# A sixth tile for split weights, operands kept split in DRAM, and PSUM reads put first in the seven products

## The chip, the cores and the metric

The kernel runs on one core of a Trainium2 chip. The metric is the time of one execution on the device in microseconds (us), the median of three runs. The five engines of the core have queues of their own and meet at semaphores: TensorE (PE; its weight loads are PEld), VectorE (DVE), ScalarE (ACT), GpSimd (POOL) and SyncE (SP, which here only issues transfers). Matmuls accumulate in eight PSUM banks.

## What is computed

A decoder layer over 2048 tokens of width 1024, in float32. Two branches (a gated DeltaNet with four heads, a sliding-window attention with eight query heads) read one normalized projection; their outputs are merged by gates, and a SwiGLU feed-forward of inner width 2816 follows:

```python
merged = gates[:, :, 0] * (y_dn @ w_branch_dn[l]) + gates[:, :, 1] * (y_swa @ w_branch_swa[l])
x = x + merged @ w_out[l]
h2 = rms_norm(x, ffn_norm[l])
x = x + (jax.nn.silu(h2 @ w_gate[l]) * (h2 @ w_up[l])) @ w_down[l]
```

The change lies in the feed-forward: `h2 @ w_gate` and `h2 @ w_up`, and the tiles through which all weights come.

## The kernel before

**Blocks.** The 2048 tokens are worked off in four blocks of 512. Each block goes through projections with the DeltaNet cores beside them (`mixer`), the output projection (`wo`), and the feed-forward. The next block's attention projections and its attention (`window_start`, `swa`) run inside the feed-forward of the block before, so that VectorE and ACT have their work there too.

**Split operands.** A product of float32 is made of three matmuls of a narrower type: hi times hi, hi times lo, lo times hi. A raw weight half of 128 x 512 is loaded into a `wraw` tile (256 KB, `load_raw`, L159), ACT makes its `hi` (L169), and VectorE or POOL, in turn, its `lo` by a subtraction (L170); the two stand in one `whl` tile. In block 0 the split weights of most products are also stored to DRAM (`wk<-whl`, 512 KB, L182), and blocks 1 to 3 load them back ready (`load_kept`, `whl<-wk`, L187), without `wraw` and without a split. There are eight `wraw` and five `whl` tiles; a tile is filled when the one that used its buffer before has been read.

**Feed-forward units.** The 22 units of 128 inner columns are grouped in five parts (4, 4, 4, 4, 6 units); after each part the down product adds its share. Block 0 uses plain products (`ffn_eight`): gate with A11 and A12, up with A21 and A22 (quarters of the two weight units), and in `four` it also makes the sums S1 to S4 of these quarters (VectorE and POOL, L229, tile `ws`), which are stored raw. Blocks 1 to 3 use Strassen's scheme with seven products of half size (`ffn_seven`), in the order S2, A11, S1, S3, A12, A22, S4; block 3 does its first two units plainly (`PLAIN`). Each of the seven operands is loaded raw and split each time it is used (`seven`).

**Chained banks.** The seven products share three PSUM banks, Y, G and Z. Y gets S2*T2, is copied to `c[:, 1]` by ACT (`pc<-acc`), gets S3*T3 on top, is read by VectorE into `U[:, 1]` (`pu<-pc,acc`), and then A22*T4 is added. So PE may not start A22 before `pu` is read. In the same way the second use of G waits for a `pc` copy, and that of Z for `up<-pu,acc`.

**What sets the order.** PE's order is written out at build time by a driver with a rough estimate of times: the dense products in program order, with steps of the side chains (attention, DeltaNet, norms) put in when they should be ready. The other engines' lists are ordered by a scheduler by priority, program order and readiness; side steps are emitted with a priority of 300. `refill` loads the next block's normalized activations `h` back at the beginning of the last part's down product (`h<-hk`, sixteen transfers on ACT's queue); they had been parked in DRAM by `window_start`.

Line numbers are those of the profile. Most operations are recorded through one helper and have its line, L110; they are told apart by their tiles.

Of the kernel before, what the change touches and what calls it, by code (L numbers as in the profile page):

```python
# [8 lines left out]
F32 = mybir.dt.float32  # L9
F32R = mybir.dt.float32r  # L10
I32 = mybir.dt.int32
AF = mybir.ActivationFunctionType
ALU = mybir.AluOpType
# [6 lines left out]
TB = 512  # L20
# [7 lines left out]
FSPLIT = (4, 4, 4, 4, 6)  # L28
NU = 60
ND = 6  # L30
WR = 8
WB = 5
PLAIN = 2
PSUB = 2
LANES = 2
GATES_AT = 2
# [79 lines left out]
class Emitter:  # L116
# [40 lines left out]
    def load_raw(self, src, n=TB):  # L157
        raw = self.wp.tile([P, 528], F32, name="wraw", tag="wraw", bufs=WR)
        self.raw.sync.dma_start(out=raw[:, :n], in_=src)  # L159
        return raw[:, :n]  # L160

    def either(self):
        self.nsub += 1
        return self.raw.vector if self.nsub > 6 and self.nsub % PSUB else self.raw.gpsimd

    def split_raw(self, r, n=TB):
        t = self.wp.tile([P, 2, 528], F32R, name="whl", tag="whl", bufs=WB)
        hi, lo = t[:, 0, :n], t[:, 1, :n]
        self.raw.scalar.activation(hi, r, AF.Copy)  # L169
        self.either().tensor_tensor(out=lo, in0=r, in1=hi, op=ALU.subtract)  # L170
        return t
# [13 lines left out]
    def load_kept(self, d, n=TB):  # L185
        t = self.wp.tile([P, 2, 528], F32R, name="whl", tag="whl", bufs=WB)
        self.raw.sync.dma_start(out=t[:, :, :n].bitcast(F32), in_=d)  # L187
        return t
# [20 lines left out]
    def quad(self, keys, m, h):  # L209
        return self.w_all[UNITS[keys[m]]][:, h * TB:(h + 1) * TB]  # L210

    def four(self, keys):

        v, gp = self.raw.vector, self.raw.gpsimd
        got = {n: self.load_raw(self.quad(keys, m, h))
               for n, m, h in (("A11", 0, 0), ("A12", 0, 1), ("A21", 1, 0), ("A22", 1, 1))}
        self.store_kept()

        def group(m):
            hl = [[t[:, e, :TB].rearrange("p (a m) -> p a m", a=4) for e in range(2)]  # L220
                  for t in [self.split_raw(got["A%d%d" % (m + 1, h + 1)]) for h in range(2)]]
            return lambda k: (hl[k // 4][0][:, k % 4], hl[k // 4][1][:, k % 4])

        def sums():
            kept = self.kept[keys] = {}
            for n, x, y, op, eng in (("S1", "A21", "A22", ALU.add, v), ("S2", "S1", "A11", ALU.subtract, v),
                                     ("S3", "A11", "A21", ALU.subtract, gp), ("S4", "A12", "S2", ALU.subtract, gp)):
                got[n] = self.u([TB], name="ws")
                eng.tensor_tensor(out=got[n], in0=got[x], in1=got[y], op=op)  # L229
                kept[n] = self.keep(got[n], [TB])  # L230
        return group, sums

    def seven(self, keys):

        own = {"A11": (0, 0), "A12": (0, 1), "A22": (1, 1)}
        self.store_kept()

        def of(name):
            t = self.split_raw(self.load_raw(self.quad(keys, *own[name]) if name in own else self.kept[keys][name]))
            return [t[:, e, :TB].rearrange("p (a m) -> p a m", a=4) for e in range(2)]  # L240
        return of

# [777 lines left out]
    def ffn_up(self, b, H, hs, f):  # L1020

        keys = (("up", f, 0), ("up", f, 1))
        if b == 0:
            group, sums = self.four(keys)
        elif b + 1 == self.nblocks and f < PLAIN:
            group, sums = lambda m: self.raw_weights(keys[m]), lambda: None
        else:
            return self.ffn_seven(H, keys)
        return self.ffn_eight(hs, group, sums)
# [28 lines left out]
    def ffn_seven(self, H, keys):  # L1058


        nc, v, gp = self.nc, self.nc.vector, self.nc.gpsimd
        yield lambda: len(H) == 4
        w = self.seven(keys)
        half = (slice(0, 256), slice(256, 512))
        bank = lambda: self.acc()[:, 0:256]
        Y = bank()
        yield from self.product(Y, w("S2"), H, "T2")
        c = self.u([2, 256], name="pc")
        nc.scalar.activation(c[:, 1], Y, AF.Copy)
        G = bank()  # L1070
        yield from self.product(G, w("A11"), H, "B11")
        nc.scalar.activation(c[:, 0], G, AF.Copy)
        U = self.u([2, 256], name="pu")
        gp.tensor_tensor(out=U[:, 0], in0=c[:, 0], in1=c[:, 1], op=ALU.add)
        Z = bank()
        yield from self.product(Z, w("S1"), H, "T1")
        yield from self.product(Y, w("S3"), H, "T3", start=False)
        v.tensor_tensor(out=U[:, 1], in0=c[:, 0], in1=Y, op=ALU.add)
        th = self.u([TB], name="th")
        up = self.u([TB], name="up")  # L1080
        v.tensor_tensor(out=up[:, half[1]], in0=U[:, 1], in1=Z, op=ALU.add)
        yield from self.product(G, w("A12"), H, "B21", start=False)
        nc.scalar.activation(th[:, half[0]], G, AF.Tanh, scale=0.5)
        v.scalar_tensor_tensor(out=th[:, half[0]], in0=th[:, half[0]], scalar=1.0, in1=G, op0=ALU.add, op1=ALU.mult)
        yield from self.product(Y, w("A22"), H, "T4", start=False)
        v.tensor_tensor(out=up[:, half[0]], in0=c[:, 0], in1=Y, op=ALU.add)
        yield from self.product(Z, w("S4"), H, "B22", start=False)
        v.tensor_tensor(out=U[:, 0], in0=U[:, 0], in1=Z, op=ALU.add)
        nc.scalar.activation(th[:, half[1]], U[:, 0], AF.Tanh, scale=0.5)
        v.scalar_tensor_tensor(out=th[:, half[1]], in0=th[:, half[1]], scalar=1.0, in1=U[:, 0], op0=ALU.add, op1=ALU.mult)  # L1090
        v.tensor_tensor(out=th, in0=th, in1=up, op=ALU.mult)
        return self.ffn_act(th)
# [7 lines left out]
    def window_start(self, b, hs):  # L1100
        yield lambda: len(hs) == KT
        yield from self.skv(b, hs)
        yield from self.sq(b, hs)
        if b:

            self.put = []
            for k, h in enumerate(hs):
                self.put.append([])
                for e in range(2):
                    d = self.kp.tile([P, TB], F32, name="hk", tag="hk%d_%d" % (k, e))  # L1110
                    nc = self.raw
                    nc.scalar.dma_start(out=d, in_=h[e].bitcast(F32))
                    self.put[-1].append(d)
            hs.clear()

    def refill(self, hs):
        for d in self.put:
            h = self.pair("h")
            for e in range(2):
                self.raw.scalar.dma_start(out=h[e].bitcast(F32), in_=d[e])  # L1120
            hs.append(h)
            yield 1500
# [45 lines left out]
    def program(self):  # L1168
        nc, v = self.nc, self.nc.vector
        hs = []  # L1170
        self.bias_ready = False
        self.spawn(self.norm1(0, hs))
        self.spawn(self.band_bias())
        yield from self.window_start(0, hs)
        for b in range(self.nblocks):
            hs = yield from self.mixer(b, hs)
            more = b + 1 < self.nblocks
            x1 = []
            self.spawn(self.load_x(b, x1, 4000))
            yield lambda: len(x1) == NT  # L1180

            def addx(half, t, ps):
                v.tensor_tensor(out=x1[t][half], in0=x1[t][half], in1=ps, op=ALU.add)
            yield from self.tok_gemm(("wo",), [self.mt.pop(m) for m in range(KT)], addx)
            h2, h4 = [], []
            self.spawn(self.norm2(b, x1, h4, h2))
            if more:
                yield from self.window_start(b + 1, hs)
            f = 0
            for part, nf in enumerate(FSPLIT):  # L1190
                acts = []
                for _ in range(nf):
                    acts.append((yield from self.ffn_up(b, h4, h2, f)))
                    f += 1
                last = part == len(FSPLIT) - 1
                if last and more:
                    h2.clear()
                    h4.clear()
                    self.spawn(self.refill(hs))

                def addf(half, t, ps):
                    addx(half, t, ps)
                    if last:
                        r = slice(b * TB + t * P, b * TB + (t + 1) * P)
                        nc.scalar.dma_start(out=self.out[r, half * TB:(half + 1) * TB], in_=x1[t][half])
                yield from self.tok_gemm(("down", part), acts, addf)
# [101 lines left out]
```

## Time and profile before

| | us |
|---|---|
| Median of three runs (lowest, highest) | 3213.54 (3211.43, 3216.75) |
| The profiled execution | 3212.49 |
| Its span, from first to last instruction | 3210.7 |
| PE busy | 3054.8 (95%) |
| DVE, ACT, POOL busy | 1831.4 (57%), 1174.2 (37%), 876.8 (27%) |
| DMA, mean over the span | 181 GB/s, 579.75 MB |

PE is busy nearly all the time, so what the other engines do counts only where PE waits for it. The view of waits names for each wait of an engine the instruction or transfer that came last. The timeline gives single instructions in order of time, those of one kind in a row merged, with the idle time in front of them in brackets. The view of windows gives for a stretch the busy time of each engine, the granted clock of TensorE (1.00 is the full speed of 2.4 GHz, 0.50 the lower level of 1.2 GHz) and the mean share of the 16 DMA engines. Blocks 1, 2 and 3 have their seven-product stages from about 1328, 2110 and 2880 us on; the plain units of block 0 lie between 527 and 899 us.

### The profile page before, as it was taken

To read this page: it belongs to the slowest core of one execution; us is meant where nothing else is said; L and a number is where in the kernel's file an instruction comes from. 1 tells how busy PE (TensorE), PEld (TensorE's weight loads), DVE (VectorE), ACT (ScalarE), POOL (GpSimd) and SP (SyncE) were. 2 spreads that over 40 slices of the span, in tenths; PEclk is the share of its full clock that TensorE was granted. 3 is DMA by queue.
4 is the path that set the end of the run, shared out by engine and by line. 5 is a ranking of instruction groups with operands and counts; after the bars stand their busy time and mean duration, and the time that the engine had idled before them with its cause. 6 is when DMAs were issued, how large, how long until landed. Compare 5 with 4: busy or idle time off the path is not lost. (4 is left out here: it accounts for less than half of the span.)

```text
span 3210.7 us, 47669 instructions
## 1 busy us (share of the span) xinstructions
PE 3054.8 (95%) x17158; PEld 2594.7 (81%) x17158; DVE 1831.4 (57%) x4258; ACT 1174.2 (37%) x2804; POOL 876.8 (27%) x773
## 2 busy tenths in 40 slices
PE   6889989999999999889999999989999999989999
PEld 5677878778878887878997888787889788879898
DVE  5866656644437644766554564486555646445554
ACT  4444334523223322554341333255334232233343
POOL 2433211544412100344341110053423201023232
PEclk9999999999999999999999999999999999999999
DMA  7553584466684447434657445743556644536555
GB/s 245 194 177 134 182 299 144 145 216 219 214 315 150 132 138 263 132 120 158 197 178 260 138 138 171 237 135 106 190 178 230 202 129 145 170 110 203 178 178 174
DMA packets 305589, 579.75 MB, mean 181 GB/s; under 512 B 25503, under 2 KB 26696, under 8 KB 305352
## 3 DMA queue, kind: packets, MB, share of 16 engines
q1 hardware_dynamic: 277520, 527.28, 50.0%
q10 hardware_dynamic: 27832, 49.42, 4.3%
q8 instruction: 135, 2.21, 0.3%
q14 instruction: 102, 0.84, 0.1%
HBM read 452.79 MB, written 123.81 MB: 180 GB/s over the span
## 5 line engine op out<-in xcount | busy, mean ns | idle before, releaser
L110 PE MATMUL acc<-h,whl 128*128 128x512 f32 (+1 forms) x4944 | 1140.2, 383 | 5.4 <-DVE whl L170 1.8
L110 PEld LDWEIGHTS acc<-h,whl 128*128 128x128 f32 x4944 | 872.3, 190 | 179.5 <-issue 3.3
L170 POOL TENSOR_TENSOR whl<-wraw,whl 128x512 fp32r<-128x512 f32 (+1 forms) x351 | 473.9, 1352 | 1128.0 <-ACT whl L169 975.9
L169 ACT ACTIVATE whl<-wraw 128x512 fp32r<-128x512 f32 (+1 forms) x696 | 432.9, 629 | 609.1 <-PE acc L110 438.5
L110 PE MATMUL acc<-hb,whl 128*128 128x256 f32 x4656 | 577.3, 282 | 22.7 <-DVE pu L110 12.6
L110 PEld LDWEIGHTS acc<-hb,whl 128*128 128x128 f32 x4656 | 561.4, 190 | 32.4 <-DVE pu L110 17.9
L110 PE MATMUL acc<-whl,a 128*128 128x512 f32 x2112 | 503.8, 397 | 23.2 <-DMA whl<-wk 16.9
L110 PEld LDWEIGHTS acc<-whl,a 128*128 128x128 f32 x2112 | 395.7, 189 | 122.1 <-DMA whl<-wk 24.8
L170 DVE TENSOR_TENSOR whl<-wraw,whl 128x512 fp32r<-128x512 f32 x345 | 303.4, 880 | 207.4 <-ACT whl L169 189.1
L110 DVE TENSOR_TENSOR x<-x,acc 128x512 f32<-128x512 f32 x192 | 131.5, 686 | 288.6 <-PE acc L110 287.8
L110 PE MATMUL acc<-whl,mt 128*128 128x512 f32 x768 | 182.8, 399 | 8.3 <-DVE h L110 5.9
L110 PEld LDWEIGHTS acc<-whl,mt 128*128 128x128 f32 x768 | 145.7, 191 | 44.4 <-DVE h L110 6.9
L110 DVE SCALAR_TENSOR_TENSOR cv<-xr,cst_sb,cv 128x512 f32<-128x512 f32 x144 | 133.1, 924 | 59.5 <-ACT cv L110 55.6
L110 PE MATMUL acc<-whl,h 128*128 128x264 f32 (+1 forms) x768 | 141.8, 344 | 0.0
L110 PEld LDWEIGHTS acc<-whl,h 128*128 128x128 f32 x768 | 120.1, 191 | 17.5 <-issue 1.1
L110 POOL COPY ccar<-xr 128x3 f32<-128x3 f32 x48 | 9.0, 188 | 374.1 <-ACT xr L110 374.1
L110 PE MATMUL acc<-sp,whl 128*128 128x512 f32 x384 | 101.8, 405 | 0.0
L110 POOL TENSOR_TENSOR hs<-hf 128x256 f32<-128x256 f32 x12 | 12.6, 1050 | 320.6 <-ACT hf L110 320.6
L110 POOL TENSOR_TENSOR pT<-pT,cst_sb 128x512 f32<-128x512 f32 x62 | 88.1, 1446 | 40.8 <-ACT pT L110 40.8
L110 ACT ACTIVATE L<-L,ast 128x256 f32<-128x256 f32 (+1 forms) x192 | 83.7, 457 | 39.6 <-DVE ast L110 39.5
L110 PE MATMUL acc<-ydn,whl 128*128 128x512 f32 x384 | 93.2, 402 | 0.2
L110 DVE SCALAR_TENSOR_TENSOR th<-th,acc 128x256 f32<-128x256 f32 (+1 forms) x88 | 43.3, 492 | 78.7 <-ACT th L110 78.5
(209 smaller groups left out, 3478.7 us busy)
## 6 DMA issues: line engine op xcount, KB each, us to landing
whl<-wk SPq DMA_DIRECT2D x444, 512.0 KB, 4.0
wraw<-in_w_all SPq DMA_DIRECT2D x436, 256.0 KB, 3.7
wk<-whl SPq DMA_DIRECT2D x148, 512.0 KB, 4.0
wraw<-wk SPq DMA_DIRECT2D x256, 256.0 KB, 2.7
wk<-ws SPq DMA_DIRECT2D x88, 256.0 KB, 2.2
x<-in_x ACTq DMA_DIRECT2D x56, 256.0 KB, 5.0
hk<-h ACTq DMA_DIRECT2D x48, 256.0 KB, 5.1
h<-hk ACTq DMA_DIRECT2D x48, 256.0 KB, 6.2
```

What stands on the lines that cost most here:

```text
L110: r = f(*args, **kw)
L169: self.raw.scalar.activation(hi, r, AF.Copy)
L170: self.either().tensor_tensor(out=lo, in0=r, in1=hi, op=ALU.subtract)
```

## The change

- `WB` goes from 5 to 6 and `WR` from 8 to 6: one more `whl` tile, two fewer `wraw` tiles (a `whl` tile is twice as large, so the memory is the same).
- In block 0, `four` also stores the split A11, and for the first 12 of the 22 units A12 and A22 too (`ready`, `BUSY`). `seven` loads these back ready in blocks 1 to 3; the other operands are split as before.
- Four reads of the chained banks in `ffn_seven` (two `pc`, one `pu`, one `up`) are emitted with a priority of 600.
- `refill` pauses 6000 ns of the driver's estimate before its first load. Two further lines (`if b > 0`, `if True`) say the same as before.

```diff
-WR = 8
-WB = 5
+WR = 6
+WB = 6
 PLAIN = 2
+BUSY = 12
+READS = 600
...
-    def four(self, keys):
+    def four(self, keys, ready):
...
+        kept = self.kept[keys] = {}
+
         def group(m):
-            hl = [[t[:, e, :TB].rearrange("p (a m) -> p a m", a=4) for e in range(2)]
-                  for t in [self.split_raw(got["A%d%d" % (m + 1, h + 1)]) for h in range(2)]]
+            hl = []
+            for h in range(2):
+                n = "A%d%d" % (m + 1, h + 1)
+                t = self.split_raw(got[n])
+                if n in ready:
+                    kept[n] = self.keep(t[:, :, :TB].bitcast(F32), [2, TB])
+                hl.append([t[:, e, :TB].rearrange("p (a m) -> p a m", a=4) for e in range(2)])
...
         def of(name):
-            t = self.split_raw(self.load_raw(self.quad(keys, *own[name]) if name in own else self.kept[keys][name]))
+            kept = self.kept[keys].get(name)
+            if name in own and kept is not None:
+                t = self.load_kept(kept)
+            else:
+                t = self.split_raw(self.load_raw(self.quad(keys, *own[name]) if name in own else kept))
...
-            group, sums = self.four(keys)
+            group, sums = self.four(keys, ("A11", "A12", "A22") if f < BUSY else ("A11",))
...
-        nc.scalar.activation(c[:, 1], Y, AF.Copy)
+        with self.tc.high_priority(READS):
+            nc.scalar.activation(c[:, 1], Y, AF.Copy)
...
-        v.tensor_tensor(out=U[:, 1], in0=c[:, 0], in1=Y, op=ALU.add)
+        with self.tc.high_priority(READS):
+            v.tensor_tensor(out=U[:, 1], in0=c[:, 0], in1=Y, op=ALU.add)
...
     def refill(self, hs):
+        yield 6000
         for d in self.put:
```

PE's list is the same in both kernels, in kind and order. The lists of the other engines move. VectorE's list at the first unit of seven products in block 1: `qst` and `qr` are the statistics and the scaling of the attention queries, `whl` a split, `pu` and `up` the reads of the banks Y and Z. Before:

```order
1569 L110 SCALAR_TENSOR_TENSOR qst<-qst 128x32 x2
1570 L110 TENSOR_TENSOR qr<-qr,qst 128x512 x4
1571 L110 TENSOR_TENSOR eg<-eg 128x16
1572 L110 TENSOR_SCALAR eg<-eg 128x16
1573 L110 TENSOR_TENSOR pu<-pc,acc 128x256
1574 L170 TENSOR_TENSOR whl<-wraw,whl 128x512
1575 L110 TENSOR_TENSOR up<-pu,acc 128x256
```

The same place in the changed kernel (its helper has line 112, its split line 172):

```order
1572 L172 TENSOR_TENSOR whl<-wraw,whl 128x512
1573 L112 SCALAR_TENSOR_TENSOR qst<-qst 128x32 x2
1574 L112 TENSOR_TENSOR qr<-qr,qst 128x512 x2
1575 L112 TENSOR_TENSOR pu<-pc,acc 128x256
1576 L112 TENSOR_TENSOR qr<-qr,qst 128x512
1577 L112 TENSOR_TENSOR up<-pu,acc 128x256
1578 L112 TENSOR_TENSOR qr<-qr,qst 128x512
1579 L112 TENSOR_TENSOR eg<-eg 128x16
1580 L112 TENSOR_SCALAR eg<-eg 128x16
```

`pu` moved in front of two of the four `qr` and of both `eg`; the statistics still stand ahead of it.

SP's list at the beginning of block 1's feed-forward, where `wraw` rows are raw loads for a later split and `whl` rows load ready pairs. Before:

```order
314 L187 DMA whl<-wk 128x2x512 x8
315 L159 DMA wraw<-in_w_all 128x512
316 L159 DMA wraw<-wk 128x512 x2
317 L159 DMA wraw<-in_w_all 128x512 x2
318 L159 DMA wraw<-wk 128x512 x2
```

And in the changed kernel:

```order
318 L189 DMA whl<-wk 128x2x512 x9
319 L161 DMA wraw<-wk 128x512 x3
320 L189 DMA whl<-wk 128x2x512 x2
321 L161 DMA wraw<-wk 128x512
322 L189 DMA whl<-wk 128x2x512
323 L161 DMA wraw<-wk 128x512 x2
```

Three of seven loads of a unit became loads of a ready pair, which wait for a `whl` buffer and stand between the raw loads.

ACT's list at the end of block 0's feed-forward, where `a<-th` ends the last unit and `h<-hk` is the reload. Before:

```order
482 L169 ACTIVATE whl<-wraw 128x512 x3
483 L110 ACTIVATE a<-th 128x512
484 L1120 DMA h<-hk 128x512 x16
485 L169 ACTIVATE whl<-wraw 128x512 x4
486 L1205 DMA out<-x 128x512 x2
```

And in the changed kernel:

```order
476 L171 ACTIVATE whl<-wraw 128x512 x2
477 L112 ACTIVATE a<-th 128x512
478 L1137 DMA h<-hk 128x512 x16
479 L171 ACTIVATE whl<-wraw 128x512 x6
480 L1223 DMA out<-x 128x512 x4
```

The reload stands at the same place; one split that stood in front of it now stands behind it.

## Rows read from the trace of the kernel before

**Rows 1.** The page, part 1: the span, and the busy time of the engines.

```profile
span 3210.7 us, 47669 instructions
...
PE 3054.8 (95%) x17158; PEld 2594.7 (81%) x17158; DVE 1831.4 (57%) x4258; ACT 1174.2 (37%) x2804; POOL 876.8 (27%) x773
```

**Rows 2.** Waits of PE over the span: total us, times, longest.

```profile
PE acc L110 <- DMA whl<-wk: 17.9, 18, 2.2
PE acc L110 <- DVE pu L110: 12.6, 7, 5.2
PE aux L110 <- DVE qT L110: 9.5, 10, 1.3
...
PE acc L110 <- ACT whl L169: 8.4, 4, 6.1
...
PE acc L110 <- ACT pc L110: 4.0, 5, 1.6
PE acc L110 <- POOL whl L170: 3.5, 6, 0.9
```

**Rows 3.** Timeline of DVE near 1335 us: start, us, instruction, [idle before].

```profile
1330.72 2.09 DVE L110 TENSOR_SCALAR qst<-qst 128x32 f32<-128x32 f32 x3
...
1335.09 0.18 DVE L110 TENSOR_TENSOR qst<-qst 128x32 f32<-128x32 f32 x1
...
1337.38 2.50 DVE L110 TENSOR_TENSOR qr<-qr,qst 128x512 f32<-128x512 f32 x4
...
1339.96 0.41 DVE L110 TENSOR_TENSOR pu<-pc,acc 128x256 f32<-128x256 f32 x1
```

**Rows 4.** Timeline of POOL, same stretch.

```profile
1330.57 1.29 POOL L170 TENSOR_TENSOR whl<-wraw,whl 128x512 fp32r<-128x512 f32 x1 [1.02 <-ACT whl L169]
```

**Rows 5.** Timeline of PE, 1340 to 1500 us.

```profile
1340.43 10.80 PE L110 MATMUL acc<-hb,whl 128*128 128x256 f32 x75 [5.15 <-DVE pu L110]
...
1383.39 0.96 PE L110 MATMUL acc<-whl,a 128*128 128x512 f32 x3 [1.69 <-DMA whl<-wk]
1385.58 5.76 PE L110 MATMUL acc<-whl,a 128*128 128x512 f32 x18 [1.22 <-DMA whl<-wk]
```

**Rows 6.** Windows: busy (instructions) by engine PE, PEld, DVE, ACT, POOL; clock; DMA share, GB/s.

```profile
1340.00:1345.00 5.00, 4.57 (x24) 4.57 (x25) 2.75 (x7) 0.63 (x1) 0.00 (x0) 0.59 0.18 52
1385.00:1390.00 5.00, 4.42 (x13) 3.57 (x14) 0.69 (x1) 0.09 (x1) 0.00 (x0) 0.66 0.54 209
699.27:743.92 44.65, 44.65 (x194) 36.24 (x193) 17.98 (x27) 14.08 (x24) 23.24 (x17) 1.00 0.59 195
743.92:766.09 22.17, 22.17 (x98) 18.03 (x97) 10.29 (x13) 5.70 (x9) 3.90 (x3) 1.00 0.78 272
1501.24:1541.37 40.13, 39.99 (x338) 39.65 (x337) 25.69 (x41) 21.09 (x43) 20.41 (x17) 1.00 0.60 189
1690.00:1710.00 20.00, 19.84 (x86) 15.70 (x85) 2.75 (x4) 0.00 (x0) 0.00 (x0) 1.00 1.05 393
```

**Rows 7.** The page, part 5: the splits (busy us, mean ns, idle before).

```profile
L170 POOL TENSOR_TENSOR whl<-wraw,whl 128x512 fp32r<-128x512 f32 (+1 forms) x351 | 473.9, 1352 | 1128.0 <-ACT whl L169 975.9
L169 ACT ACTIVATE whl<-wraw 128x512 fp32r<-128x512 f32 (+1 forms) x696 | 432.9, 629 | 609.1 <-PE acc L110 438.5
...
L170 DVE TENSOR_TENSOR whl<-wraw,whl 128x512 fp32r<-128x512 f32 x345 | 303.4, 880 | 207.4 <-ACT whl L169 189.1
```

**Rows 8.** DMA issues of 1501 to 1541 us: count, KB each, median us to landing.

```profile
whl<-wk SPq DMA_DIRECT2D x4, 512.0 KB, 4.6
```

**Rows 9.** DMA of 1375 to 1385 us: packets, MB, share; issues.

```profile
q1 hardware_dynamic: 1362, 2.58, 79.9%
...
whl<-wk SPq DMA_DIRECT2D x5, 512.0 KB, 7.3
```

**Rows 10.** Timeline of ACT near 900 us.

```profile
900.16 16.33 ACTq L1120 DMA_DIRECT2D h<-hk  x16
916.54 2.19 ACT L169 ACTIVATE whl<-wraw 128x512 fp32r<-128x512 f32 x4 [15.81 <-DMA h<-hk]
```

More of the change, by code (lines that the diff above doesn't have):

```diff
@@ L217, in four @@
         self.store_kept()
+        kept = self.kept[keys] = {}
         def group(m):
-            hl = [[t[:, e, :TB].rearrange("p (a m) -> p a m", a=4) for e in range(2)]
-                  for t in [self.split_raw(got["A%d%d" % (m + 1, h + 1)]) for h in range(2)]]
+            hl = []
[5 more added lines that the diff above has]
+                hl.append([t[:, e, :TB].rearrange("p (a m) -> p a m", a=4) for e in range(2)])
             return lambda k: (hl[k // 4][0][:, k % 4], hl[k // 4][1][:, k % 4])
         def sums():
-            kept = self.kept[keys] = {}
             for n, x, y, op, eng in (("S1", "A21", "A22", ALU.add, v), ("S2", "S1", "A11", ALU.subtract, v),
@@ L1068, in ffn_seven @@
         c = self.u([2, 256], name="pc")
-        nc.scalar.activation(c[:, 1], Y, AF.Copy)
+        with self.tc.high_priority(READS):
+            nc.scalar.activation(c[:, 1], Y, AF.Copy)
         G = bank()
         yield from self.product(G, w("A11"), H, "B11")
-        nc.scalar.activation(c[:, 0], G, AF.Copy)
+        with self.tc.high_priority(READS):
+            nc.scalar.activation(c[:, 0], G, AF.Copy)
         U = self.u([2, 256], name="pu")
@@ L1077, in ffn_seven @@
         yield from self.product(Y, w("S3"), H, "T3", start=False)
-        v.tensor_tensor(out=U[:, 1], in0=c[:, 0], in1=Y, op=ALU.add)
+        with self.tc.high_priority(READS):
+            v.tensor_tensor(out=U[:, 1], in0=c[:, 0], in1=Y, op=ALU.add)
         th = self.u([TB], name="th")
         up = self.u([TB], name="up")
-        v.tensor_tensor(out=up[:, half[1]], in0=U[:, 1], in1=Z, op=ALU.add)
+        with self.tc.high_priority(READS):
+            v.tensor_tensor(out=up[:, half[1]], in0=U[:, 1], in1=Z, op=ALU.add)
         yield from self.product(G, w("A12"), H, "B21", start=False)
@@ L1103, in window_start @@
         yield from self.sq(b, hs)
-        if b:
+        if b > 0:
             self.put = []
@@ L1198, in program @@
                     h4.clear()
-                    self.spawn(self.refill(hs))
+                    if True:
+                        self.spawn(self.refill(hs))
                 def addf(half, t, ps):
```

## The prediction, made before the changed kernel ran

> **What bounds the kernel now.** I read the page's first part first: TensorE is busy 3054.8 of 3210.7 us, so at most 156 us of this span is not matmul time [rows 1]. PE's list of instructions is word for word the same before and after the change, in kind and order, so the change can only move those 156 us and the clock. Then the waits of PE by releaser: the change touches five of them, on the kept operands' loads (17.9), on the reads `pu` (12.6), on ACT's half of a split (8.4), on the copies `pc` (4.0) and on POOL's half (3.5), 46.4 us in all [rows 2]. 6.1 of ACT's 8.4 is one wait in block 0, in front of which ACT sat behind sixteen reload transfers of `h` [rows 10]. The reader is to see in PE's timeline what the other waits look like: 5.15 us in front of the A22 product, then 1.69 and 1.22 us at the first two tiles of the down product [rows 5].
>
> **The reads.** At 1340 us in block 1 PE waits for `pu`. VectorE works through the statistics of the attention queries first: three small operations that start at 1330.72 take 2.09 us, then more of them and four `qr` of 2.50 us together, and only at 1339.96 comes `pu` [rows 3]. The lists show that the change puts `pu` in front of the last two `qr` and both `eg`, not in front of the statistics (the order in the section on the change). That is 1.25 us and some 0.16 us by the same rows. Second, the four `qs` on ACT and the four reductions now follow one another without a split between them; I take 0.7 us, about one ACT split [rows 7]. Third, the twelve small operations need about 0.2 us each where nothing else runs (0.18 at 1335.09), 2.5 us in all, and took about 6.0 us up to 1337.38, without the split among them; the first three ran beside a POOL split that started at 1330.57 [rows 3, 4]. So some 3.5 us were lost beside POOL. Now three of seven operands of a unit need no split, and I give back half: 1.7 us.
> The Trainium skill, SBUF — State Buffer, Who interferes with whom, has VectorE and GpSimd share one pair of ports as an exclusive lock, for the whole instruction. The trace agrees (2.09 us for three against 0.18 for one). By it the 1.7 is earned only where a POOL split is really gone from beside the chain; without that, the wait would shrink by 2.1 us and not by 3.8.
> Sum: 5.15 falls by 3.8 to about 1.3 us, in blocks 1 and 2 alike: 7.6, and 0.9 of the smaller `pu` waits: 8.5 us. Bounds: 2.8 (the order alone, twice 1.4) and 12.6.
>
> **The sixth whl tile.** A tile is loaded or split when PE has finished with the tile that used the buffer before. With five tiles that is four tiles ahead, with six, five. A product of seven takes 40.13/28 = 1.43 us, a down tile 22.17/8 = 2.77 [rows 6]. So the first down tile after the seven products starts 7.15 us ahead and no longer 5.7, and inside a down product each has 2.77 us more. The 18 waits on `whl<-wk` are 2.2 us at the longest [rows 2]; the worst place is the pair 1.69 + 1.22 [rows 5], of which 1.43 goes at least. SP's queue is also less often held up there by raw loads that wait for a split. I take 13.5 of 17.9 us. Bounds: 5 (if the landings of rows 9 become the rule) and 17.9.
>
> **Fewer splits.** ACT's list has 696 splits before and 564 after: 46 less in blocks 1 and 2, 40 in block 3. That is 132 x 0.629 us of ACT, 66 x 1.35 of POOL and 66 x 0.88 of VectorE [rows 7]; nearly all lies beside matmuls and counts nothing. On PE's path it counts where PE waits for a split outside that one wait of block 0: 2.3 (ACT) + 3.5 (POOL), of which I take half, 3. The `pc` copies are put ahead of attention's copies on ACT: 2.5 of 4.0. Bounds for both: 0 and 9.8.
>
> **The clock behind the long waits.** After the 5.15 us the granted clock is at its lower level (1.2 GHz) for a while: in 1340 to 1345 us 24 matmuls take 4.57 us, where 24 x 0.119 = 2.9 is the pace at 2.4 GHz; in 1385 to 1390, 13 of the wide ones take 4.42 and not 3.0 [rows 6]. That is 1.7 + 1.4 in block 1, and as much in block 2: 6.2 us, which goes if the waits in front become short. I take 4.5; bounds 0 and 6.2.
>
> **What the change costs.** (a) The reload of `h`: the added pause of 6000 moves no instruction. The sixteen transfers stand on ACT where they stood, and ACT is held for 16.33 us [rows 10]. But one split less is done in front of them (232 against 233), so PE runs dry one tile earlier, 3 matmuls of 0.23: 1 us with its follow-up; bounds 0 and 6.
> (b) Block 0 stores 46 more pairs of 512 KB. For units 0 to 11 the transfers now take per unit 0.59 x 44.65/4 = 6.6 us of the DMA engines, plus three stores: at 393 GB/s and a share of 1.05, 1.4 each: 10.8 of 11.2 us, and with the down product (0.78 x 22.17) 60.5 of 66.8 [rows 6]. It fits, narrowly; loads in block 0 are issued six or more tiles ahead. 2 us; bounds 0 and 8.
> (c) In blocks 1 to 3 three loads of 512 KB take the place of three of 256 KB: 6.0 us of DMA per unit become 8.1 of 10.0, a share of 0.81. They cover 4.6 us at a share of 0.6 [rows 6, 8] and 7.15 are there. 3 us; bounds 0 and 30 (rivals).
> (d) What is late next: PE then comes sooner to attention's own chain; the waits on `qT` (9.5 us [rows 2]) have nothing to do with weights and grow when PE is early. 5 us; bounds 0 and 8.
> The smaller raw pool (six for eight) I cost at nothing: raw loads are still issued some 15 us or ten products ahead, since only four of seven operands use it; without that cover it would come back as ACT waits on `wraw`.
>
> **Sum.** 8.5 + 13.5 + 3 + 2.5 + 4.5 = 32 gained, 1 + 2 + 3 + 5 = 11 lost: 21 us. The profiled execution took 3212.49 us (span 3210.7 and 1.8 around it); 3191.5, and the median of the runs lies 1.05 above it: 3192 us.
>
> **Rivals.**
> More goes (chance 0.14): all the five waits but the one of block 0, 40 us, and the clock's 6.2, with half of the costs: 3173. For it: PE waits in few places, and two changes help each. Against it: pairs of long waits end in chains that stay.
> Nothing much (0.16): the statistics in front of `pu` still decide, and the loads come as late as before because each is larger. Then 2.8 + 5 + 2 = 10 gained and 11 lost: 3214. For it: `pu` stays behind the whole chain of small operations in VectorE's list.
> Slower (0.11): the kept loads land late. In a ring of six a kept tile's load may take five products, 7.15 us; each us beyond costs one per unit, and 34 units of blocks 1 to 3 have three of them (12 + 12 + 10). At a DMA share of 0.80 five such loads in a row took 7.3 us [rows 9], and the steady share will be 0.81. At 7.9 us the gain is used up; at 8.2 it is 34 x 1.05 = 36 us, less the 3 counted: 3225. Against it: those five were issued almost at once after a held queue, while here two come 1.4 us apart, and in steady stretches they took 4.6 [rows 8].
> That the reload does nothing is part of the forecast.
>
> **How the numbers follow.** The forecast has 0.57, the rest 0.02. What this measurement can tell from no change is about 0.2%, 6.4 us. Faster by more: 0.57 + 0.14 and a little of the third case, 0.74; within: 0.14; slower: 0.12. The forecast's own range is 3182 to 3202; the one given leaves out the slow case and the far end of the large one: 3178 to 3212.
>
> **What would show it.** Waits on `pu` at about 4 us in all and the ones at 1340 and 2122 us down to 1 to 2; waits on `whl<-wk` at about 4; the clock at 1.00 there; ACT splits at 564; still a wait of 6 to 8 us near 917 us; a DMA share near 0.8 in the seven products of units 0 to 11, and 512 KB landing in 5 to 6 us. Wrong: PE waits on `whl<-wk` inside the seven products, on stores in block 0, or a `pu` wait above 3.5 us.

## The result, and the profile after

The changed kernel takes 3162.63 us (median of four runs, 3157.99 to 3165.03), the one before, run beside it, 3213.60: a ratio of 0.9839, 95% interval 0.9822 to 0.9856, or 51 us faster. The forecast was 3192 us with 3178 to 3212 as its range. The direction was right; the gain is more than twice the 21 us forecast and the time lies below the range. The rival in which more goes gave 3173, and even that is too long.

The page of the changed kernel, part 1, which answers to [rows 1]:

```profile
span 3156.2 us, 47296 instructions
...
PE 3024.1 (96%) x17158; PEld 2579.2 (82%) x17158; DVE 1756.2 (56%) x4192; ACT 1100.6 (35%) x2672; POOL 803.6 (25%) x707
```

The span is 54.5 us shorter. The profiled execution is the fastest of the four, and its mean granted clock is 0.989 where the other three have 0.986 and 0.987, so the stretches below flatter the change by some 5 us. PE's idle time fell from 155.9 to 132.1 us, that is by 23.8. The other 30.7 us are busy time of PE, with the same 17158 matmuls: they ran at a faster pace. More than half of the gain is thus in a place where the view of PE's waits shows nothing.

The waits of PE in the changed kernel, against [rows 2]; total us, times, longest:

```profile
PE acc L112 <- ACT whl L171: 8.9, 2, 8.0
...
PE acc L112 <- DVE pu L112: 7.1, 4, 2.2
...
PE aux L112 <- DVE qT L112: 6.1, 7, 1.6
...
PE acc L112 <- ACT pc L112: 4.0, 3, 1.6
...
PE acc L112 <- DMA whl<-wk: 0.7, 3, 0.3
...
PE acc L112 <- POOL whl L172: 0.3, 1, 0.3
```

The waits on `whl<-wk` are gone (17.9 to 0.7), those on `pu` fell by 5.5 and not by 8.5, `pc` is where it was, and `qT`, which was to grow by 5, fell by 3.4. All the waits that the change touches gave back 25.4 us.

Where the time went, by stretches of equal work of PE: blocks 0 to 3, from the first matmul of each to the first of the next, in the kernel before (us of the stretch, then busy us of PE, PEld, DVE, ACT, POOL; clock; DMA share, GB/s).

```profile
12.77:940.78 928.01, 863.44 (x4102) 695.97 (x4103) 541.49 (x1295) 359.75 (x854) 315.98 (x255) 0.97 0.59 204
940.78:1722.27 781.49, 752.57 (x4509) 652.40 (x4508) 452.93 (x1066) 288.09 (x702) 197.44 (x180) 0.99 0.54 175
1722.27:2506.30 784.03, 752.83 (x4509) 652.04 (x4508) 452.26 (x1066) 288.02 (x702) 197.88 (x180) 0.99 0.53 174
2506.30:3210.70 704.40, 685.98 (x4041) 594.25 (x4039) 380.71 (x804) 232.13 (x528) 165.15 (x153) 1.00 0.51 162
```

The same four in the changed kernel:

```profile
12.13:940.56 928.43, 859.60 (x4103) 693.52 (x4103) 547.20 (x1295) 360.55 (x854) 323.47 (x255) 0.97 0.66 230
940.56:1696.61 756.05, 739.17 (x4510) 645.04 (x4509) 423.24 (x1043) 262.63 (x656) 168.18 (x157) 1.00 0.60 198
1696.61:2455.30 758.69, 742.20 (x4510) 647.57 (x4508) 422.94 (x1043) 262.31 (x656) 168.11 (x157) 1.00 0.59 195
2455.30:3156.20 700.90, 683.16 (x4041) 593.04 (x4039) 358.85 (x784) 208.92 (x488) 143.44 (x133) 1.00 0.55 178
```

Block 0 is as long as before (+0.4 us), blocks 1 and 2 are shorter by 25.4 and 25.3 us, block 3 by 3.5. In block 1, 13.4 of the 25.4 us are busy time of PE and 12.0 idle time.

Three stretches of block 1 show what such busy time is. In the kernel before, then in the changed one (columns as above):

```profile
1306.36:1327.56 21.20, 21.20 (x92) 17.24 (x91) 17.77 (x27) 14.84 (x29) 11.49 (x11) 0.92 0.36 113
...
1373.93:1396.40 22.47, 19.39 (x109) 15.25 (x108) 9.91 (x15) 5.95 (x14) 9.60 (x8) 0.92 0.60 199
...
1685.78:1722.27 36.49, 34.08 (x146) 26.78 (x145) 7.05 (x11) 1.05 (x2) 0.00 (x0) 1.00 0.95 341
```

```profile
1304.85:1324.52 19.67, 19.67 (x93) 16.12 (x91) 18.31 (x27) 14.62 (x28) 11.68 (x11) 1.00 0.35 108
...
1366.13:1383.41 17.28, 17.28 (x110) 14.20 (x108) 6.71 (x13) 4.60 (x12) 6.82 (x7) 1.00 0.77 261
...
1663.32:1696.61 33.29, 33.29 (x147) 27.01 (x146) 7.04 (x11) 1.05 (x2) 0.00 (x0) 1.00 1.04 384
```

The first has no idle time in it and gained 1.5 us, by a granted clock of 0.92 that is 1.00 now. That is no work of the change: in both kernels PE waits 2.99 us directly in front of the stretch, and the clock fell to its lower level behind that wait in the one profiled execution and not in the other.

```profile
1305.95 0.66 PE L110 MATMUL aux<-cst_sb,xn 128*128 128x128 f32 x4 [2.99 <-ACT hf L110]
```

```profile
1304.43 0.66 PE L112 MATMUL aux<-cst_sb,xn 128*128 128x128 f32 x4 [2.99 <-ACT hf L112]
```

The second stretch gained 5.2 us: 3.1 of idle time, and 2.1 of busy time at a clock that rose from 0.92 to 1.00. The third gained 3.2 us at a clock of 1.00 in both: 2.4 of idle time, and 0.8 that PE's row calls busy. Time of that last kind shows in the view of the weight loads' waits, which I had not read. Before, then after:

```profile
PEld acc L110 <- DMA whl<-wk: 26.6, 24, 2.7
...
PEld acc L110 <- DVE pu L110: 17.9, 19, 5.4
```

```profile
PEld acc L112 <- DVE pu L112: 7.9, 4, 2.4
...
PEld acc L112 <- DMA whl<-wk: 2.5, 5, 0.7
```

The transfers cost the weight loads 26.6 us where the matmuls' row has 17.9 [rows 2], and `pu` 17.9 where it has 12.6. The two fell by 24.1 and 10.0 us; in PE's rows by 17.2 and 5.5. So 8.7 and 5.3 us lie between the two views before the change. The time lost lies between them too: in the third stretch PE's view has 2.4 us of these waits and the weight loads' 3.7, and the stretch became 3.2 us shorter. The Trainium skill, Perfetto Trace Analysis, Tensor Engine Instruction, says that TensorE's end is estimated by the profiler and not observed. These rows fit that: the beginning of a wait can be counted as busy time of the matmul before it.

The statistics in front of `pu`, [rows 3], look like this on VectorE in the changed kernel:

```profile
1326.73 1.71 DVE L112 TENSOR_SCALAR qst<-qst 128x32 f32<-128x32 f32 x3
...
1332.63 1.29 DVE L112 TENSOR_TENSOR qr<-qr,qst 128x512 f32<-128x512 f32 x2
1333.84 0.41 DVE L112 TENSOR_TENSOR pu<-pc,acc 128x256 f32<-128x256 f32 x1
```

`pu` stands in front of the last two `qr`, as read from the lists, and the first three small operations still take 1.71 us beside a POOL split. PE's wait there is 2.15 us and no longer 5.15. The clock of the stretch around it was 0.85 and is 1.00 (before, then after), and the pair of waits in front of the down product [rows 5] is gone:

```profile
1327.56:1351.07 23.51, 18.36 (x140) 18.14 (x139) 18.11 (x34) 10.72 (x24) 8.71 (x8) 0.85 0.38 113
```

```profile
1324.52:1343.20 18.68, 16.53 (x140) 16.32 (x139) 15.59 (x33) 7.70 (x18) 5.72 (x5) 1.00 0.72 223
```

```profile
1334.31 2.97 PE L112 MATMUL acc<-hb,whl 128*128 128x256 f32 x23 [2.15 <-DVE pu L112]
...
1373.32 5.03 PE L112 MATMUL acc<-whl,a 128*128 128x512 f32 x21
```

The wait of block 0 near 917 us is still there and is longer, 8.05 for 6.1 us, with ACT held by the reload for 17.64 us [rows 10]:

```profile
898.20 17.64 ACTq L1137 DMA_DIRECT2D h<-hk  x16
915.89 3.23 ACT L171 ACTIVATE whl<-wraw 128x512 fp32r<-128x512 f32 x6 [17.06 <-DMA h<-hk]
```

### The profile page after: what moved, and what is told of

Its sections match the earlier page's. It is cut to its first block, busy times and chain, and to the rows that moved or that the text cites. A ratio compares the mean times of both kernels' runs of the same rounds, so it can differ in the third digit from the quotient of the medians.

```text
span 3156.2 us, 47296 instructions
## 1 busy us (share of the span) xinstructions
PE 3024.1 (96%) x17158; PEld 2579.2 (82%) x17158; DVE 1756.2 (56%) x4192; ACT 1100.6 (35%) x2672; POOL 803.6 (25%) x707
## 5 line engine op out<-in xcount | busy, mean ns | idle before, releaser
L172 POOL TENSOR_TENSOR whl<-wraw,whl 128x512 fp32r<-128x512 f32 (+1 forms) x285 | 387.8, 1363 | 1181.8 <-ACT whl L171 1041.8
L112 PE MATMUL acc<-hb,whl 128*128 128x256 f32 x4656 | 565.3, 280 | 11.1 <-DVE pu L112 7.1
L171 ACT ACTIVATE whl<-wraw 128x512 fp32r<-128x512 f32 (+1 forms) x564 | 352.3, 629 | 577.4 <-PE acc L112 255.2
L172 DVE TENSOR_TENSOR whl<-wraw,whl 128x512 fp32r<-128x512 f32 x279 | 232.1, 832 | 265.7 <-ACT whl L171 252.4
L112 DVE SCALAR_TENSOR_TENSOR a<-th,a 128x512 fp32r<-128x512 f32 x88 | 85.0, 966 | 63.2 <-ACT a L112 62.3
```

Source lines behind the costliest of these rows:

```text
L112: r = f(*args, **kw)
```

## The experiments

All times are medians; the kernel before, run beside each, lies between 3211.6 and 3214.6, and the ratios are to it. The first seven runs take the change apart: pools (six and six for eight raw and five `whl`), reads first, kept operands.

**The pools alone.** Against the kernel before:

```diff
-WR = 8
-WB = 5
+WR = 6
+WB = 6
```

> The kernel before with only the pools changed: six buffers for raw operands and six for whl (WR 6, WB 6); same splits, same kept operands, same order of the reads. Theory A (the sixth tile does most of it): the waits on whl<-wk fall from 17.9 to under 3 us, the low-clock stretches behind them at 1385 and 1432 us in block 1 and at 2166 and 2214 in block 2 go, about 5 us in front of the down product and 5 in it per block: 3213 - 22 = about 3191. Theory B (the fewer splits do most of it, the ring is only the room they need): waits on whl<-wk fall by about 5, 3207. Both: the wait of 5.15 us on pu at 1340 stays, with its clock.

Measured: 3181.97 us, ratio 0.9900 (0.9886 to 0.9914), 32.6 us faster: theory A, and half as much again as it expected. PE's waits on `whl<-wk` fall from 17.9 to 1.3 us, the weight loads' from 26.6 to 5.3. The mean granted clock is 0.984 as before, and yet part of the gain is busy time again: 11.5 us of it, beside 14.8 of idle time.

```profile
span 3184.4 us, 47482 instructions
...
PE 3043.3 (96%) x17158; PEld 2591.1 (81%) x17158; DVE 1810.0 (57%) x4258; ACT 1176.1 (37%) x2804; POOL 886.2 (28%) x773
```

Against both theories, the `pu` wait near 1334 us falls to 1.80 without any change of priorities, because VectorE's list, which follows from when buffers come free, is another one too. And a new wait appears:

```profile
1430.91 1.44 PE L110 MATMUL acc<-hb,whl 128*128 128x256 f32 x5 [4.83 <-ACT pc L110]
```

In this kernel ACT's copies `pc` stand behind the operation `a<-th`, which waits for VectorE. VectorE's timeline in front of it, with the two splits and the products `th`:

```profile
1422.40 2.39 DVE L170 TENSOR_TENSOR whl<-wraw,whl 128x512 fp32r<-128x512 f32 x2
1424.72 1.53 DVE L110 SCALAR_TENSOR_TENSOR th<-th,pu 128x256 f32<-128x256 f32 x1
1426.28 1.63 DVE L110 TENSOR_TENSOR th<-th,up 128x512 f32<-128x512 f32 x1
```

and POOL's at that time:

```profile
1422.73 4.63 POOL L170 TENSOR_TENSOR whl<-wraw,whl 128x512 fp32r<-128x512 f32 x3 [7.01 <-ACT whl L169]
```

Three POOL splits in a row run beside these operations.

**The reads alone.** The changed kernel with `WR = 8`, `WB = 5`, `BUSY = 0` and `()` for `("A11",)`, so that only the four priorities are left.

> The kernel before with only the reads put first (READS 600); eight raw and five whl buffers, no kept A11, A12, A22. Theory A (order decides): the pu waits at 1340 and 2122 us fall from 5.15 to about 2.2 each and the low clock behind that of block 1 goes, as in the changed kernel: 2 x 3 + 1.7 + 1.5 of the pc copies, some 9 us, 3204. Theory B (the POOL splits beside the statistics decide, and they are still there): the waits fall by 1.25 each, to about 3.9, the clock stays low: 2.5 to 4 us, 3210.

Measured: 3202.97, ratio 0.9961 (0.9947 to 0.9975), 11.6 us faster. The time is theory A's; the waits are between the two: `pu` 9.1 us in all, 3.2 at the longest.

**The kept operands alone.** The changed kernel with

```diff
-WR = 6
-WB = 6
+WR = 8
+WB = 5
-READS = 600
+READS = 0
```

> The kernel before with only the kept split operands (A11, A12, A22 of twelve units, A11 of the others), reads where they were, eight raw and five whl buffers. The loads of kept operands are then 5.72 us ahead and not 7.15. Theory A (the prediction's cost of late loads, with the shorter ring): 512 KB at a DMA share of 0.8 land in 5 to 7 us, waits on whl<-wk grow inside the seven products, 3220 to 3240. Theory B (fewer splits relieve ACT, VectorE, POOL and SP, and the loads are in time): waits on pu and pc fall, those on whl<-wk stay: 3213 - 8 = 3205. If the time is near 3190, the kept operands and not the ring make the gain.

Measured: 3217.99, ratio 1.0015 (1.0005 to 1.0025): 3 us slower. Part of both theories holds: `pu` and `pc` fall to 9.3 and 1.7 us, and the loads come late in forty places. In the seven products near 1500 us, 512 KB land after 5.5 us (median) and 6.8 at the longest, where five tiles give 5.72.

```profile
PE acc L112 <- DMA whl<-wk: 27.9, 40, 2.8
```

**Pools and kept operands, without the reads.** The changed kernel with `READS = 0`.

> The changed kernel with READS 0, so pool and kept operands without the reads put first. If the three parts add up, this is the changed kernel plus the reads' share: by the theory that order decides 9 us, 3172; by the theory that fewer POOL splits beside the statistics shorten pu by themselves 3 us, 3166. A wait on pu at about 1340 us of over 4 us speaks for the first, one of under 3 for the second.

Measured: 3163.13, ratio 0.9840 (0.9825 to 0.9856). The same time as with the reads first, although the `pu` wait near 1336 us is 3.52 and not 2.15: with the reads first the waits on `pu` are 2.7 us less in all, those on attention's `L` 2.6 us more, and PE's idle time is 132.1 us against 130.5 without. Neither theory had that.

**Pools and reads, nothing kept.** The changed kernel with `BUSY = 0` and `()` for `("A11",)`.

> The changed kernel without kept A11, A12, A22 (all units split them again in blocks 1 to 3): six and six buffers, reads first. The pool alone gave 32.6 us, pool and kept operands 51.4, all three 51. In the pool alone PE waits 4.83 us at 1431 us for the copy pc, which stands on ACT behind splits and attention's copies. Theory A (the kept operands gain because ACT is free for that copy sooner): with the copy put first the wait goes as well, about 12 us of the 19 come back, 3170. Theory B (ACT, VectorE and POOL need the relief all along): 3180, as the pool alone.

Measured: 3185.00, ratio 0.9910 (0.9897 to 0.9924): theory B. The `pc` wait of 4.8 us stays, priority or not, since `a<-th` in front of it waits for VectorE. So on six tiles the kept operands are worth 19 us without the reads and 22 with them.

**Kept operands and reads, with the old pools.** The changed kernel with `WR = 8`, `WB = 5`.

> The changed kernel with the old pools (eight raw, five whl): kept operands and reads first. Kept operands alone lost 3.4 us on five tiles, reads alone gained 11.6. Theory A (five tiles is the limit, kept operands need the sixth): 40 short waits on whl<-wk as in the kernel with the kept operands alone, 3206 to 3212. Theory B (effects add up): 3214.6 + 3.4 - 11.6 = 3206. Theory C (reads and kept operands help one another, the pool adds the rest): below 3195.

Measured: 3212.47, ratio 0.9998 (0.9989 to 1.0007): theory A. No gain at all without the sixth tile:

```profile
PE acc L112 <- DMA whl<-wk: 31.9, 36, 3.4
```

**The raw pool alone.** The kernel before with `WR = 6` and five `whl` buffers.

> The kernel before with six raw buffers for eight and still five whl buffers. Theory A (the raw pool is idle room, the ring of whl does the pool's 32.6 us): the same time, 3214 +- 6. Theory B (with fewer raw loads ahead SP's queue reaches the kept operands' loads sooner, and that makes the gain): 3190 to 3205, and the waits on whl<-wk below 10 us. Theory C (raw operands come late): ACT waits for wraw, over 3220.

Measured: 3216.60, ratio 1.0014 (1.0005 to 1.0024): theory A, some 4 us lost rather than nothing. The pools' gain is the `whl` ring's. (Eight raw buffers with six `whl` tiles were not run.)

These seven and the two kernels give, in us: nothing 3213, reads 3203, kept 3218, both 3212 on five tiles; nothing 3182, reads 3185, kept 3163, both 3163 on six. The parts don't add up. On five tiles kept operands cost 3 to 12 by the ratios, on six they bring 19 to 22.

**The reload of block 0 on SP's queue.**

```diff
-    def refill(self, hs):
+    def refill(self, b, hs):
         yield 6000
+        q = self.raw.sync if b == 0 else self.raw.scalar
...
-                self.raw.scalar.dma_start(out=h[e].bitcast(F32), in_=d[e])
+                q.dma_start(out=h[e].bitcast(F32), in_=d[e])
```

> The changed kernel, with the sixteen reload transfers of h in block 0 issued on SP's queue and not on ACT's. Theory A (the wait of 8.0 us at 917 us is ACT held behind the reload): ACT goes on splitting, the wait and the low clock behind it go: 8.0 + 1.7 of 3.4 us at half clock, 3162.6 - 9 = 3153. Theory B (the tile is late for another reason, or SP held there makes raw weights late): the wait stays between 4 and 8 us or moves to wraw, 3158 to 3166.

Measured: 3159.51, ratio 0.9834 (0.9820 to 0.9847), no measurable difference to the changed kernel. The wait is 6.12 us, now for raw weights behind the reload: theory B.

**The reload between the splits.** `tok_gemm` of the last down product takes three steps of `refill` per tile, so that ACT's list alternates; `refill` is no longer spawned and loses its pauses. The edit does this in every block that has a next one, not in block 0 alone.

```diff
                 w = self.weights(key + (half, u), 2)
+                for _ in range(3 if reload else 0):
+                    next(reload, None)
```

> The changed kernel with the sixteen reload transfers of h issued in ACT's list between the splits of the last down product of block 0, three per tile, and not all in front of them. In the changed kernel the transfer engines are at a share of 1.05 from 904 to 922 us, and with the reload on SP the wait at 917 only fell from 8.05 to 6.1 us. Theory A (the queue in front of the splits makes the wait, wherever the queue is): the wait falls below 3 us and the low clock behind it goes, 3162 - 8 = 3154. Theory B (the transfer engines are full, 4.2 MB at 400 GB/s are 10.5 us wherever they stand): the wait falls by less than 3 us or comes back later, before 940 us, 3158 to 3164.

Measured: 3160.89, ratio 0.9840 (0.9826 to 0.9855): theory B. The wait at 917 is down to 0.24, and one of 4.83 us comes right behind the product, in front of the next block's first matmuls:

```profile
935.27 10.04 PE L112 MATMUL acc<-h,whl 128*128 128x512 f32 x33 [4.83 <-DMA whl<-wk]
```

in a stretch where the transfer engines are full:

```profile
930.00:940.00 10.00, 5.17 (x13) 3.78 (x13) 0.69 (x1) 0.00 (x0) 0.00 (x0) 0.66 1.05 407
```

With the share at 1.05 in all three kernels and a wait left in each, the limit is the bytes rather than the queue: the prediction's reading of [rows 10] named the place and not the limit. A run with fewer bytes there was not made.

**Seven tiles.** The changed kernel with `WR = 4`, `WB = 7`.

> The changed kernel with seven whl buffers and four raw ones. Waits on whl<-wk are 0.7 us with six. Theory A (six is enough, the term is used up): same time, 3162 +- 5, if four raw buffers are enough. Theory B (each tile more lets PE run through other lateness too): 3150 to 3157. Theory C (four raw buffers are too few; PE waits for splits, ACT for wraw): over 3170.

Measured: 3173.67, ratio 0.9877 (0.9862 to 0.9892): theory C. No wait on `whl<-wk` is left, but waits on POOL's halves come to 8.6 us and `pc` to 7.0.

**Everything kept.** The changed kernel with `BUSY = 22`.

> The changed kernel with A11, A12 and A22 kept for all 22 units (BUSY 22; in the changed kernel ten units keep A11 alone). Block 0 stores 20 pairs of 512 KB more and blocks 1 to 3 do some 60 splits less. Theory A (stores in block 0 fit beside the loads, fewer splits go on gaining): units 12 to 21 of blocks 1 and 2 lose no time to splits in the changed kernel already, so 3155 to 3162. Theory B (the prediction's cost of stores: units of block 0 run at a DMA share near 1): block 0 gets longer by 0.5 to 1 us for each of ten units, 3167 to 3175.

Measured: 3168.29, ratio 0.9864 (0.9848 to 0.9881). 6 us slower than the changed kernel, as theory B has it, though not in the units of block 0: waits on `whl<-wk` are back at 6.4 us, nearly all in the down products of blocks 1 to 3, and the wait at the reload is 11.1 us for 8.05.

**All lo halves on VectorE.** The changed kernel with

```diff
-PSUB = 2
+PSUB = 100000
```

> The changed kernel with all lo halves of the splits but the first six on VectorE; POOL does none (PSUB 100000). VectorE gets some 280 splits more. Theory A (POOL beside VectorE is what stretches the chains: 0.69 us operations take 1.5): the 1.36 us of a POOL split become 0.7 on VectorE and the neighbours run at their own pace, pu waits fall again: 3155 or less. Theory B (VectorE is the next to be late; the relief in the changed kernel came from fewer splits and not from which engine does them): waits on pu, qT and whl<-DVE grow, 3165 to 3185.

Measured: 3126.25, ratio 0.9731 (0.9717 to 0.9746), 36 us faster than the changed kernel: theory A. The split of 1363 ns on POOL and 832 on VectorE now takes 742:

```profile
L172 DVE TENSOR_TENSOR whl<-wraw,whl 128x512 fp32r<-128x512 f32 x558 | 410.6, 742 | 238.7 <-ACT whl L171 230.6
```

VectorE is busy only 96 us longer (1852.4) with 279 splits more. The profiled span is 32.0 us shorter, and 24.5 of these come in block 0, where every operand is split:

```profile
12.20:916.10 903.90, 853.13 (x4103) 689.67 (x4103) 584.96 (x1412) 361.77 (x854) 160.05 (x138) 0.98 0.67 236
```

against 928.43 in the changed kernel. The Trainium skill, SBUF — State Buffer, Who interferes with whom, says that VectorE and GpSimd share one pair of ports as an exclusive lock, held for a whole instruction. The traces agree: the `th` that took 1.63 us beside POOL's splits in the kernel with the pools alone takes 0.69 here, at 1397 us. How much of the 36 us is this and how much POOL's own slower split is not told apart.

Still open was whether the pools' 32.6 us are the ring's depth or the other order of the lists beside POOL, and by which way the kept operands gain. Four kernels with the same edit of `PSUB`:

**Pools alone, on VectorE.**

> The kernel before with six and six buffers and all lo halves of the splits on VectorE; nothing kept, reads not first. The kept operands gave 19 us on top of the six tiles, 12 of them at 1431 and 2200 us, where with the pool alone VectorE's products th took 1.5 us beside three POOL splits. Theory A (the kept operands gain because POOL splits go from beside VectorE): with no POOL split at all those places are short here too, and the time is near that of the changed kernel with all splits on VectorE, 3126 to 3134. Theory B (they gain because ACT and VectorE have fewer operations in front of PE's): the 19 us stay, 3140 to 3148.

Measured: 3132.54, ratio 0.9752 (0.9739 to 0.9766): theory A. With POOL out of the way the kept operands (with the reads) are worth 6.3 us and not 19. The two `th` there:

```profile
1399.84 0.43 DVE L110 SCALAR_TENSOR_TENSOR th<-th,pu 128x256 f32<-128x256 f32 x1
...
1400.78 0.70 DVE L110 TENSOR_TENSOR th<-th,up 128x512 f32<-128x512 f32 x1
```

0.43 and 0.70 us for 1.53 and 1.63, and the wait for `pc` behind them is 2.01 for 4.83.

**The kernel before, on VectorE.**

> The kernel before with all lo halves of the splits on VectorE, five whl buffers, nothing else changed. Theory A (the waits on whl<-wk come from the ring of five alone and have nothing to do with POOL): they stay at 16 to 20 us, and the time is some 25 us above that with six tiles, about 3160. Theory B (the sixth tile's 32 us were mostly another order of VectorE's and ACT's lists beside POOL): with POOL out of the way five tiles cost little, 3135 to 3145.

Measured: 3163.63 (3152.87 to 3173.97, the widest spread of all), ratio 0.9840 (0.9818 to 0.9862): theory A. The waits on `whl<-wk` stay, 19.8 us, and the sixth tile is worth 31 us (by the ratios 28, some 8 either way) with POOL away, as with it there. This one line, alone on the kernel before, brings 48 us, nearly as much as the whole change.

**Kept operands and reads on five tiles, on VectorE.**

> Kept operands, reads first and all lo halves on VectorE, but eight raw and five whl buffers. Theory A (a kept load needs more than the 5.72 us that five tiles give): 30 us of waits on whl<-wk as in the changed kernel with the old pools, and the sixth tile is worth 40 to 50 us here too: 3126 + 45 = 3171. Theory B (part of those waits were tiles set free late by POOL): 3145 to 3155.

Measured: 3159.98, ratio 0.9840 (0.9822 to 0.9858), between the theories: the sixth tile is worth 34 us here and 50 with POOL's splits. `whl<-wk` still has 24.2 us.

**The reload between, on VectorE.**

> The changed kernel with all lo halves on VectorE and the reload of h issued between the splits of block 0's last down product. With POOL's splits the reload between them gave 0 to 3 us. The one on VectorE alone has 3126.2 and a wait of 6.3 us on ACT's split at the reload. If the transfer engines are what is full there: 3123 to 3127; if the split was: 3118 to 3121.

Measured: 3125.12, ratio 0.9726 (0.9713 to 0.9739), as without it: the transfer engines are full there. This and the kernel with all lo halves on VectorE are the fastest, 86 us below the kernel before.

## Why the prediction was wrong

**The step that failed: gains were priced from PE's idle time.** The prediction says that the change "can only move those 156 us and the clock", and its sum puts prices on PE's waits. Idle time fell by 23.8 us in the profiled executions. Another 30.7 us came out of PE's busy time, for which the sum had 4.5 us of clock.

**The sixth whl tile** is the term that was mis-sized most. "I take 13.5 of 17.9 us. Bounds: 5 (if the landings of rows 9 become the rule) and 17.9." It measures 32.6 us alone, 31.1 with POOL's splits away, and 50 under kept operands. The mechanism was right (a tile more is 1.43 or 2.77 us more lead, and the waits vanish), and in PE's own row the term came nearly as priced: 17.9 us became 1.3. But that row was not the time lost. With the pools alone PE's busy time fell by 11.5 us at the same mean clock of 0.984. The weight loads' view has 26.6 us for the same transfers, of which 21.3 went. That is a better bound and still below 32.6, and not all of a weight load's wait is lost time, so the rest of the busy time is not located. The order of the lists moved too: `pu` got shorter and `pc` longer. How much of the 32.6 us is order and how much depth is not settled, since the pool changes both.

**Kept operands: their sign depends on the ring.** The prediction gave fewer splits 3 and took 3 for late loads. On five tiles the second was too small: 27.9 us of waits, 10 more than before. On six it was nothing, 0.7. The steady share of about 0.8 came as worked out (0.81 in the same products as [rows 8]), but 512 KB land in about 5 us and 7.15 are there, so the rival with late loads had the right mechanism on the wrong side of its own threshold. The gain was 19 to 22 and not 3, because I counted only PE's direct waits on splits. What POOL's splits do to VectorE's operations I had read from [rows 3, 4] and used for `pu` alone; at 1431 and 2200 us they stretch `th`, and with it ACT's queue and the copy `pc`. Some 13 of the 19 us go when VectorE does POOL's splits.

**The clock.** I took 4.5 of 6.2 us from two places per block. The trace of the kernel before has the lower level in nineteen places, five of them in block 1, for 105.8 us in all, in which PE is busy for 82.0; in the changed kernel it is 68.5 us with 52.6 busy, and none in block 1. At half the pace half of the busy time is lost, 41 and 26 us. By this estimate 15 us of the profiled difference are clock and 16 are busy time at full clock, which no term had. The places were there to be read before. But part of the 15 is luck of the profiled execution, as the same wait of 2.99 us at 1306 us and the clocks of the other three executions show. What decides whether the clock falls behind a wait stays open.

**The reads.** 8.5 was forecast; alone they bring 11.6, on top of the rest nothing that can be measured. The order of VectorE's list near `pu` was read rightly from the lists, but the pools move it too, so I put to the priorities what the sixth tile does by itself.

**What was right.** The reload's pause moves nothing in the lists (it was not run apart), and the wait near 917 us stays, 8 us and 2 longer, where the cost was put at 1. Block 0 is as long as before, but 3.1 us longer than with the pools alone (928.4 against 925.3), of which the wait near 917 us has 1.1 us, so the 2 us for stores are about what they cost. ACT's splits are 564. **What did not come:** the waits on `qT`, forecast 5 longer, are 3.4 shorter, and the 3 us for late loads. **What was put at nothing:** six raw buffers for eight cost some 4 us on five tiles.

In the profiled executions the change brought 54.5 us, and the forecast of 21 lacks 33.5 of them: 7 in idle time (16.5 forecast, 23.8 measured), 10 in the clock, and 16 in busy time at full clock. The weight loads' view goes the same way as the last, with 11.4 us more than PE's view for the two kinds of wait that shrank most; that it is the same time is argued and not shown.

## What to carry to other kernels

Before a wait is priced, its row in the weight loads' view belongs beside the matmuls' row, and so does the granted clock in every stretch, not only behind the longest waits: the bound of 17.9 us came from the matmuls' row alone, where the weight loads' had 26.6 and the tile was worth 32.6. What a clock row shows is compared over several executions before it is put down to a change. Where a transfer is made larger, its lead and its landing time are compared first: the same edit cost 3 us with a lead of 5.7 us and gained 19 with 7.15. And where VectorE and POOL share a chain, one run with all of it on VectorE is worth trying early: it was the largest single gain of this case, 48 us alone.

## What the runs showed of the hardware

- The same elementwise split took 1363 ns on POOL, 832 on VectorE with POOL at work, and 742 with all but the first six on VectorE; moving 279 of them to VectorE added 96 us to its busy time and took 36 us off the kernel. A small VectorE operation of 0.18 us took 1.28 us beside one POOL split (changed kernel, 1327.16 us).
- Behind the same wait of PE of 2.99 us the granted clock fell in one execution (0.92 over the 21 us behind it, at 1306 us in the kernel before) and stayed at 1.00 in another (1305 us in the changed kernel). Executions of one kernel differ with their mean clock: the kernel before with all lo halves on VectorE took 3152.87 us at 0.992 and 3173.97 at 0.986.
- This core moved 407 GB/s over 10 us at a share of 1.05. Transfers held up at such a share come back as a wait elsewhere when their order is changed (8.05 us at 917, or 4.83 us at 935).
